# Pinning the two products that spread the tokens' 1/rms to their place in the code, 64 products later in TensorE's order

## The chip, the cores and the metric

One core of a Trainium2 chip runs the whole program. The metric is the device time of one execution in microseconds; the time before is the median of three runs, and a profiled execution stands beside them. The core's engines each have a queue of instructions of their own: TensorE (PE, matrix products; its weight loads are listed as PEld), VectorE (DVE), ScalarE (ACT), GpSimd (POOL) and SyncE (SP), which here issues nearly all transfers.

## What is computed

One residual block over 256 tokens of 2048 channels: an RMS norm, one wide input projection, an mLSTM branch and a pooling branch, gates, projections, an RMS norm and the residual add. What matters here is how the first norm is done:

```python
def _rmsnorm(x, w):
    xf = x.astype(jnp.float32)
    y = xf * lax.rsqrt(jnp.mean(xf * xf, axis=-1, keepdims=True) + RMS_EPS)
    return (y * w.astype(jnp.float32)).astype(x.dtype)

h = _rmsnorm(x, norm_pre_w[l])
proj = jnp.einsum('bsd,de->bse', h, w_in[l])
(q, k, v, o_g, z_a, i_pre, f_pre, u_b, z_b, g_a, g_b) = _partition(proj)
```

The kernel multiplies the weights with x unnormed (only scaled by the channel weights) and multiplies each token's result by its 1/rms afterwards.

## The kernel before

Every fp32 operand is split into a high and a low part (`hi_lo`: ACT casts the high part, `wh` from `raw`, at L62; DVE subtracts it to get the low part `wl`, at L63), and each product is made of three: high with high, low with high, high with low. Weights come in tiles of 1 MB (`raw`, three buffers), two halves each; `wh` and `wl` have four buffers.

`tok_block` makes results with tokens on the partitions, `chan_block` with channels on the partitions. `chan_block` goes through two tiles, that is four halves; for each half it writes eight products of `wh` (L143) and eight of `wl` (L145) and then calls `step()`, which moves every generator in the list `side` on by one `yield`. The side work is thereby strewn between the halves in the order of the code.

The start of the kernel: the first `tok_block` (L428) has 16 steps, through which `stats()` only counts. Then `so0` is copied out of PSUM (L432), `gates()` and `pool_weights()` join the list, and eight `chan_block`s follow (L435). Meanwhile `stats()` fetches x, squares and sums it on ACT (L245), adds the sums on DVE (L249, L192) and raises them to -1/2 on POOL (L193): `rstd`, one number per token, tokens on partitions. `stats_bc()` turns it into `rstd_bc`, the same numbers along the free axis on all partitions: a diagonal matrix `dg` from the identity and `rstd` (L261, DVE), a product of a matrix of ones with it (L262, one for each half of the tokens), and a copy from PSUM (L263, DVE). `rstd_bc` is read by `half_sum` (L409), through which every result of `chan_block` goes, and by `gates()` (L298). The flag `ready` lets `pooling` and `pool_gate` begin. `rstd` itself is read by others too: L573 scales the first two tiles `g` with it on ACT.

The order in an engine's queue is not simply the order of the code. A scheduler builds it from a plan of its own: at each point it takes the instruction that stands earliest in the code among those which its plan holds ready. So an instruction may stand in a queue ahead of others that come before it in the code, when the plan had these wait for something. In the order that results, the two products of L262 (written behind eight halves of `chan_block`) stand behind two, and five of the sixteen products of `gates()` (L286, written behind ten halves) follow at once; the other eleven stand behind ten. On the chip each engine works through its queue with the waits that its operands need.

## Time and profile before

| | |
|---|---|
| median of 3 runs | 978.75 us (978.57 to 978.86) |
| the profiled execution | 978.46 us |
| its span, first to last instruction | 976.7 us |
| TensorE busy | 965.9 us (99%) |
| VectorE busy | 630.6 us (65%) |
| ScalarE busy | 495.1 us (51%) |
| GpSimd busy | 14.5 us (1%) |

The durations all come from the one profiled execution; its own time is what they add up to. A row of a timeline gives the start and the length of an instruction, or of a run of like instructions (x8), in microseconds from the start of the span, then engine, line, operation and operands; in brackets the time that the engine stood idle before it and what ended that wait. Matrix products overlap: the length of one is longer than the distance to the next.

### The profile page before, as it was taken

How to read it: one execution, taken by the hardware profiler on the slowest of the kernel's cores; microseconds unless marked ns; L12 is line 12 of the kernel's file. 1: busy time of each engine (PE TensorE's matmuls, PEld its weight loads, DVE VectorE, ACT ScalarE, POOL GpSimd, SP SyncE). 2: the span in 40 equal slices, each digit the busy share in tenths (PEclk: the TensorE clock that was granted, in tenths of full speed). 3: DMA queues.
4: the chain of work that ended last, by engine and by line, in shares of the span. 5: the costliest groups of instructions: out<-in, count | busy, mean ns of one | idle time of the engine just before them, and what ended most of it. 6: DMA issues, size and time to landing. Idle time of an engine off the chain costs nothing.

```text
span 976.7 us, 12410 instructions
## 1 busy us (share of the span) xinstructions
PE 965.9 (99%) x4785; PEld 816.4 (84%) x4785; DVE 630.6 (65%) x938; ACT 495.1 (51%) x678; POOL 14.5 (1%) x35
## 2 busy tenths in 40 slices
PE   9999999999999999999999999999999999999996
PEld 6888888888888888888888888888888888888886
DVE  7699776677766867758677686554454455455563
ACT  7756444456644665546554475444444434443451
POOL 1000000000000000000000000000000000000001
PEclk9999999999999999999999999999999999999999
DMA  9755445544455435564555544555555555567542
GB/s 355 296 187 209 173 173 177 211 172 172 157 197 207 173 134 211 172 216 136 191 191 192 196 172 168 179 207 179 178 195 193 210 172 199 189 248 268 180 167 86
DMA packets 29306, 187.74 MB, mean 192 GB/s; under 512 B 3264, under 2 KB 3648, under 8 KB 8256
## 3 DMA queue, kind: packets, MB, share of 16 engines
q1 hardware_dynamic: 28816, 183.81, 52.6%
q10 hardware_dynamic: 432, 3.15, 0.8%
q8 instruction: 37, 0.61, 0.2%
q14 instruction: 21, 0.17, 0.0%
HBM read 184.85 MB, written 2.10 MB: 191 GB/s over the span
## 4 chain that ended last, share of the span: by engine, by line
PE 60%; issue 38%; ACT 1%; POOL 0%; DMA 0%; DVE 0%; DVEq 0%; SPq 0%; POOLq 0%
PE acc L143 18%; PE acc L123 10%; PE acc L124 10%; PE acc L126 10%; PE acc L145 9%; PE sm L72 1%; PE sm L71 1%; PE sm L73 1%; ACT xw L245 0%; PE sm L286 0%; DMA xw<-in_xw 0%; PE sm L559 0%; DVE xr L677 0%; PE sm L508 0%; POOL xr L675 0%
## 5 line engine op out<-in xcount | busy, mean ns | idle before, releaser
L63 DVE TENSOR_TENSOR wl<-raw,wh 128x1024 fp32r<-128x1024 f32 x328 | 398.5, 1223 | 263.6 <-ACT wh L62 263.4
L62 ACT CAST wh<-raw 128x1024 fp32r<-128x1024 f32 x328 | 342.3, 1050 | 370.4 <-PE acc L124 251.9
L123 PE MATMUL acc<-wh,xc 128*128 128x512 f32 x640 | 251.2, 392 | 0.1
L124 PE MATMUL acc<-wh,xc 128*128 128x512 f32 x640 | 249.6, 390 | 0.0
L143 PE MATMUL acc<-xc,wh 128*128 128x512 f32 x768 | 192.5, 392 | 0.0
L126 PE MATMUL acc<-wl,xc 128*128 128x512 f32 x640 | 172.5, 389 | 0.0
L143 PEld LDWEIGHTS acc<-xc,wh 128*128 128x128 f32 x768 | 138.9, 189 | 25.6
L126 PEld LDWEIGHTS acc<-wl,xc 128*128 128x128 f32 x640 | 120.2, 188 | 25.2
L123 PEld LDWEIGHTS acc<-wh,xc 128*128 128x128 f32 x640 | 120.4, 188 | 24.7 <-ACT wh L62 1.0
L124 PEld LDWEIGHTS acc<-wh,xc 128*128 128x128 f32 x640 | 120.4, 188 | 23.9
L145 PEld LDWEIGHTS acc<-xc,wl 128*128 128x128 f32 x768 | 104.8, 190 | 7.5
L145 PE MATMUL acc<-xc,wl 128*128 128x256 f32 x768 | 107.1, 282 | 0.0
L123 PE MATMUL acc<-wh,y_h 128*128 128x512 f32 x128 | 49.8, 389 | 0.0
L124 PE MATMUL acc<-wh,y_l 128*128 128x512 f32 x128 | 49.8, 389 | 0.0
L473 DVE SCALAR_TENSOR_TENSOR cy<-pad,vec,cy 128x256 f32<-128x256 f32 x96 | 39.3, 477 | 0.0
L123 PE MATMUL acc<-wh,m_h 128*128 128x512 f32 x96 | 37.6, 391 | 0.0
L124 PE MATMUL acc<-wh,m_l 128*128 128x512 f32 x96 | 37.4, 389 | 0.0
L126 PE MATMUL acc<-wl,y_h 128*128 128x512 f32 x128 | 34.2, 389 | 0.0
L123 PEld LDWEIGHTS acc<-wh,y_h 128*128 128x128 f32 x128 | 24.0, 188 | 5.0
L124 PEld LDWEIGHTS acc<-wh,y_l 128*128 128x128 f32 x128 | 24.0, 188 | 5.0
L126 PEld LDWEIGHTS acc<-wl,y_h 128*128 128x128 f32 x128 | 24.0, 188 | 5.0
L126 PE MATMUL acc<-wl,m_h 128*128 128x512 f32 x96 | 25.7, 389 | 0.0
(197 smaller groups left out, 771.6 us busy)
## 6 DMA issues: line engine op xcount, KB each, us to landing
raw<-in_wx SPq DMA_DIRECT2D x76, 1024.0 KB, 4.7
raw<-in_wq SPq DMA_DIRECT2D x44, 1024.0 KB, 4.8
raw<-in_wpm SPq DMA_DIRECT2D x16, 1024.0 KB, 4.7
raw<-in_wo SPq DMA_DIRECT2D x16, 1024.0 KB, 4.9
raw<-in_wpp SPq DMA_DIRECT2D x8, 1024.0 KB, 4.7
xw<-in_xw SPq DMA_DIRECT2D x15, 384.0 KB, 6.0
raw<-in_wq SPq DMA_DIRECT2D x8, 512.0 KB, 8.1
xw<-in_x SPq DMA_DIRECT2D x4, 512.0 KB, 8.3
```

The lines of the kernel that those rows point to most:

```text
L62: nc.scalar.copy(hi, src)
L63: nc.vector.tensor_tensor(lo, src, hi.bitcast(F32), op=ALU.subtract)
L71: nc.tensor.matmul(ps, lh, rh, start=start, stop=False)
L72: nc.tensor.matmul(ps, ll, rh, start=False, stop=False)
L73: nc.tensor.matmul(ps, lh, rl, start=False, stop=stop)
L123: nc.tensor.matmul(ps[t], st_h(k, t), wh[:, cols], start=k == 0, stop=False)
L124: nc.tensor.matmul(ps[t], st_l(k, t), wh[:, cols], start=False, stop=False)
L126: nc.tensor.matmul(ps[t], st_h(k, t), wl[:, cols], start=False, stop=k == n - 1)
L143: nc.tensor.matmul(ps[c], wh[:, cols], xc[:, k], start=k == 0, stop=False)
L145: nc.tensor.matmul(ps[c][:, 1], wl[:, cols], xc[:, k, 0], start=False, stop=k == KT - 1)
L473: nc.vector.scalar_tensor_tensor(y, pad[:, 1 + j : 1 + j + T], cw[:, j : j + 1], y, op0=ALU.mult, op1=ALU.add)
```

## The change

`stats()` now yields once instead of three times before it calls `stats_bc()`, so the latter is traced behind six halves of `chan_block` instead of eight, and `ready` is set there too. And the first of the two products is passed to `keep_in_program_order`, which adds an edge to the instruction traced last before it on the same engine: in TensorE's queue it has to stand behind it. The edge orders the queue and is no wait on a semaphore.

```diff
@@ stats()
         rsqrt_mean(rstd, ms, D)
-        for _ in range(3):
-            yield 1
+        yield 1
         stats_bc()
         ready.append(1)
@@ stats_bc()
         for t in range(2):
             dg = sp.tile([P, P], F32, name="dg", bufs=2)
             nc.vector.tensor_scalar(dg, ident, rstd[:, t : t + 1], None, op0=ALU.mult)
-            nc.tensor.matmul(pb[:, t * P : (t + 1) * P], ones_f, dg, start=True, stop=True)
+            i = nc.tensor.matmul(pb[:, t * P : (t + 1) * P], ones_f, dg, start=True, stop=True)
+            if t == 0:
+                tc.keep_in_program_order(i)
         nc.vector.tensor_copy(rstd_bc, pb[:, :T])
```

## Rows read from the trace of the kernel before

**Rows 1.** The page's head and first part: busy time of each engine.

```profile
span 976.7 us, 12410 instructions
PE 965.9 (99%) x4785; PEld 816.4 (84%) x4785; DVE 630.6 (65%) x938; ACT 495.1 (51%) x678; POOL 14.5 (1%) x35
```

**Rows 2.** TensorE's waits, whole span: for whom, us in total, times, longest.

```profile
PE sm L262 <- DVE dg L261: 1.6, 1, 1.6
PE sm L166 <- DVE zeros L161: 1.2, 1, 1.2
```

**Rows 3.** Timeline of TensorE, 32 to 40 us.

```profile
32.10 1.11 PE L145 MATMUL acc<-xc,wl 128*128 128x256 f32 x8
34.84 0.71 PE L262 MATMUL sm<-dg,ones_f 128*128 128x128 f32 x4 [1.63 <-DVE dg L261]
35.31 1.41 PE L286 MATMUL sm<-xc,gc 128*128 128x512 f32 x5
36.55 2.00 PE L143 MATMUL acc<-xc,wh 128*128 128x512 f32 x8
38.39 1.12 PE L145 MATMUL acc<-xc,wl 128*128 128x256 f32 x8
39.34 2.00 PE L143 MATMUL acc<-xc,wh 128*128 128x512 f32 x8
```

**Rows 4.** Timeline of VectorE, 30 to 36 us.

```profile
30.79 0.67 DVE L63 TENSOR_TENSOR gc<-gw,gc 128x64 fp32r<-128x64 f32 x4 [3.96 <-ACT gc L62]
...
34.50 0.48 DVE L261 TENSOR_SCALAR dg<-ident,rstd 128x128 f32<-128x128 f32 x2 [0.82 <-POOL rstd L193]
35.59 0.42 DVE L263 COPY rstd_bc<-sm 128x256 f32<-128x256 f32 x1 [0.61 <-PE sm L262]
```

**Rows 5.** Timeline of ScalarE, 34 to 36 us.

```profile
34.50 0.72 ACT L573 ACTIVATE g<-g,rstd 128x512 f32<-128x512 f32 x1 [1.21 <-POOL rstd L193]
35.13 1.04 ACT L62 CAST wh<-raw 128x1024 fp32r<-128x1024 f32 x1
```

**Rows 6.** Transfers issued from 22.2 to 23.0: median us to landing.

```profile
raw<-in_wq SPq DMA_DIRECT2D x1, 512.0 KB, 8.2
```

**Rows 7.** Timeline of TensorE's weight loads, around 36 us.

```profile
36.32 1.81 PEld L143 LDWEIGHTS acc<-xc,wh 128*128 128x128 f32 x8
```

**Rows 8.** Timelines of ScalarE and TensorE, the kernel's first split products.

```profile
4.58 0.62 ACT L62 CAST wh<-xw 128x512 fp32r<-128x512 f32 x1 [0.78 <-DMA xw<-in_xw]
...
5.25 0.80 PE L123 MATMUL acc<-wh,xc 128*128 128x512 f32 x1
5.85 0.46 PE L124 MATMUL acc<-wh,xc 128*128 128x512 f32 x1
```

**Rows 9.** Timeline of TensorE, 52 to 62 us.

```profile
52.35 1.12 PE L145 MATMUL acc<-xc,wl 128*128 128x256 f32 x8
53.31 2.00 PE L143 MATMUL acc<-xc,wh 128*128 128x512 f32 x8
...
58.89 2.72 PE L286 MATMUL sm<-xc,gc 128*128 128x512 f32 x11
```

**Rows 10.** Timeline of VectorE, 43 to 55 us.

```profile
43.84 1.22 DVE L63 TENSOR_TENSOR wl<-raw,wh 128x1024 fp32r<-128x1024 f32 x1 [0.48 <-ACT wh L62]
44.99 0.75 DVE L409 TENSOR_TENSOR u<-u,rstd_bc 128x256 f32<-128x256 f32 x2
...
47.34 2.35 DVE L63 TENSOR_TENSOR pw_l<-raw,pw_h 128x1024 fp32r<-128x1024 f32 x2
49.61 0.68 DVE L63 TENSOR_TENSOR pd_l<-pd,pd_h 128x512 fp32r<-128x512 f32 x1
50.21 4.71 DVE L63 TENSOR_TENSOR wl<-raw,wh 128x1024 fp32r<-128x1024 f32 x4
```

**Rows 11.** Timeline of ScalarE, 47 to 50 us.

```profile
47.45 0.62 ACT L62 CAST pd_h<-pd 128x512 fp32r<-128x512 f32 x1 [1.67 <-DVE pd L379]
47.98 1.99 ACT L62 CAST wh<-raw 128x1024 fp32r<-128x1024 f32 x2
```

## The prediction

> **What bounds the kernel now.** I read the page's first part, then TensorE's waits over the whole span, then the timelines of the engines around the one wait that is left. TensorE (PE) is busy for 965.9 of 976.7 us [rows 1]; no other engine comes near. Its waits over the whole span are two: 1.2 us at the very start, and 1.6 us in front of the pair of products of line 262 [rows 2]. So whatever the change can give lies in that hole, and whatever it can cost is a new hole somewhere else.

> I call the 16 products of one half tile of `chan_block` a unit (8 of L143, then 8 of L145) and number them u1, u2, ... from 27.5 us. A unit takes 2.79 us (u3 at 36.55, u4 at 39.34), of which the L145 half, from 38.39, is 0.95. u2's L145 half starts at 32.10, so the next product could have gone at 32.10 + 0.95 = 33.05. The pair starts at 34.84: 1.79 us of PE are lost. Then come five of the sixteen gate products (L286), and u3 starts at 36.55 [rows 3]. The pair waits for `dg`, and `dg` sat waiting for `rstd`, GpSimd's power, until 34.50 [rows 4].

> **The second wait behind the first.** Does the hole close if the pair goes elsewhere? u3 needs its own `wh`. ScalarE (ACT) casts it from 35.13 to 36.17, and the entry ahead of it in ACT's queue is L573, the scaling of `g` with `rstd`: ACT stood idle for 1.21 us, from 33.29 on, for that same `rstd`, and started L573 at 34.50 [rows 5]. It did not wait for the raw tile of u3: that was issued between 22.2 and 23.0 and landed 8.2 us later, by 31.2 [rows 6]. So u3 cannot start before 36.17 wherever the pair stands, as long as ACT's order is kept, and nothing in the change touches an ACT instruction ahead of that cast. On this step the forecast turns: the `rstd` that holds the pair holds, by way of ACT's queue, the next unit too.

> That ACT does not step over L573 is read from those rows. [...]

> **The change part by part.**
> (a) The pair moves. In the code `stats_bc` ran after u8, but its products float up to behind u2; now it is traced after u6, and the edge holds the first product behind u6's last one, 64 products later. The pair takes 34.84 to 35.31, 0.47 us of PE [rows 3], and takes the same after u6, where `dg` will be 12 us old, so no wait: +0.47 at the new place.
> (b) u3's start. Its first weight load goes at 36.32 now [rows 7], behind the gate products. After a wait for ACT the nearest row is the kernel's start: cast done at 4.58 + 0.62 = 5.20, load and product at 5.25, the next product 0.60 later, at 5.85 [rows 8]. So u3's load would go at 36.17 + 0.05 = 36.22 and its second product, by that row, at 36.82, against 36.55 + 0.23 = 36.78 now: +0.04. If the first product is as quick as now, the load's 36.32 - 36.22 is won: -0.10. I take -0.05, between them.
> (c) The gate products. They were ready before the pair (`gc` is written by 31.46 [rows 4]) and yet stand behind it, so in the plan that made the order there was no idle time ahead of the pair that they could have filled; the place that opens is the pair's own. Each takes (36.55 - 35.31)/5 = 0.25 us [rows 3], so 0.47 holds two. Each one more in the hole is one fewer behind u10, where eleven stand now [rows 9]: -0.25 each. How long the pair is in the plan no row shows; between none and twice its measured length that is 0 to 4 products, 0 to -0.99. I take 2, by the measured length: -0.50.
> (d) VectorE (DVE). `rstd_bc` (L263) is copied 0.75 us after the pair starts, now at 35.59 [rows 3, 4]. The pair will start at some 47.6 (u7 starts two units ahead of u9, at 53.31 - 2 x 2.79 = 47.7 [rows 3, 9]), so the copy moves to 48.35 and ends at 48.78, 13 us later. Queued behind it are its readers: from the first L409 to the end of the chain that makes `pd` it is 44.99 to 47.34, 2.35 us [rows 10], so `pd` is ready at 51.1 instead of 47.4. On ACT its cast (0.62) waits for it, and behind that the casts of u9 and u10 [rows 11]: 51.1 + 0.62 + 1.04 = 52.8 for u9, which starts at 53.31 + 0.4 = 53.7 [rows 9]. 0.9 us to spare: 0. On DVE the `wl` of u9 now starts at 50.21 [rows 10] and is wanted by u9's L145 half, at 53.31 + (38.39 - 36.55) + 0.4 = 55.5 [rows 3, 9]. If both `pw_l` casts (2.35) and `pd_l` (0.68) stay ahead of it, it ends at 51.1 + 2.35 + 0.68 + 1.22 = 55.35: just in time; if `pw_l` is done while DVE waits (45.1 to 48.3 lies free for it), at 53.0. SP's raw tiles go into buffers that those casts free: u11's follows the `wl` of u8 (done at 45.06 now), and u11 is wanted only behind the gate products of 58.89. Cost taken: 0.
> (e) `ready` is set two steps earlier in the code, so the first `pooling` is traced two steps sooner. Its accumulators are freed by L407 and L408, which don't read `rstd_bc`, so PE gets its PSUM back as before: 0.

> Sum: -0.05 + 0.47 - 0.50 = -0.08 us. Bounds: -0.10 + 0.47 - 0.99 = -0.62, and +0.04 + 0.47 = +0.51. The profiled execution took 978.46 (the span 976.7 and 1.76 around it); the median of the three runs is 978.75, 0.29 above. 978.46 - 0.08 + 0.29 = 978.67; I write 978.7, with a range of its own, the bounds, of 978.1 to 979.3.

> **Rivals.**
> 1. The hole closes. If ACT's order comes out with the cast of u3 ahead of L573 (its tile landed by 31.2, ACT is free at 33.29 [rows 5, 6]), `wh` is there at 34.35, gate products bridge 33.05 to then, and all 1.79 us are won: 978.75 - 1.79 = 976.95. The same if some nine or more gate products fill the hole. For it: the data is there. Against it: the plan put L573 first though it stands far later in the code, so in the plan the tile was not there yet, and no edit changes that. This is also about the ceiling: PE has no other hole.
> 2. One product stays. The edge is on `t == 0` alone. If the second product may go ahead of the first, it stands where the pair stands and waits for the second `dg`, done at 34.50 + 0.48 = 34.98, 0.14 later than PE's start there now: the hole stays, 978.75 + 0.1 = 978.85. Against it: both write the same tile `pb`, and they stand in code order now.
> 3. Slower, through DVE. The copy of `rstd_bc` waits at DVE until 48.35 for the pair. If the plan puts the `wl` of u8 (now begun at 43.84 [rows 10]) behind the copy, its readers and `pw_l`, it ends at 48.78 + 2.35 + 2.35 + 0.68 + 1.22 = 55.4, and u8's L145 wants it at 52.35 + 0.4 = 52.7 [rows 9]: PE stands 2.7 us, 978.7 + 2.7 = 981.4. It decides once more than 52.7 - 48.78 - 1.22 = 2.7 us of other DVE work stands between the copy and that cast. Against it: that cast begins 3.9 us ahead of u7 now. A smaller stall of the kind would still count as no change.

> **How the numbers follow.** A difference under 0.2% (1.96 us) is about what a measurement of this kernel cannot tell from none. Forecast 0.68; hole closed 0.15; one product stays 0.08; slower through DVE, or through another queue that the new plan orders worse, 0.09. Forecast and rival 2 hold 0.76, so the range reaches to the closed hole, with 0.15 of spread between runs: 976.8 to 979.3. The closed hole lies 0.17 us inside the limit for faster (976.79); I give 0.03 of its 0.15 to the far side. Faster 0.03, same 0.68 + 0.08 + 0.12 = 0.88, slower 0.09.

> **What would show it.** In the profile after: L262 in PE's order behind 96 products of `chan_block`, with no wait in front; some seven L286 behind u2, nine behind u10; PE idle from about 34.8 to 36.2, put down to ACT's `wh` and no longer to `dg`; L573 still ahead of u3's cast; u3 within 0.15 us of 36.55; L263 near 48.4, with DVE waiting for PE before it, some of that filled by `pw_l`; no other wait on PE. It is wrong if u3 starts near 34.8 (rival 1), if an L262 stands at 35 (rival 2), or if PE waits for a `wl` or `wh` between 47 and 60 us (rival 3).

## The result, and the profile after

The changed kernel takes 981.43 us (median of 14 executions, 979.73 to 982.41), the kernel before 978.72 (14, 978.21 to 979.39); ratio 1.0024, 95% interval 1.0016 to 1.0032. It is slower by 0.24%, against a forecast of no change at 978.7 and a range that ended at 979.3. The slower rival put the time almost there (981.4), but by a mechanism that is not in the trace.

The executions of the changed kernel fall into two groups: five from 979.73 to 980.28 with a granted clock of 0.998 over the span, and nine from 980.98 to 982.41 with 0.995 to 0.997. The profiled one (981.44, span 979.7) belongs to the second.

TensorE's waits over the whole span, to be read against [rows 2]:

```profile
PE acc L143 <- ACT wh L62: 3.0, 1, 3.0
PE sm L166 <- DVE zeros L161: 1.2, 1, 1.2
```

The wait of the pair (L261 in this kernel) for `dg` is gone. In its place stands one nearly twice as long, of u3's first product for ScalarE's `wh`. The timeline of TensorE, against [rows 3] and [rows 9]:

```profile
32.14 1.11 PE L145 MATMUL acc<-xc,wl 128*128 128x256 f32 x8
36.25 3.42 PE L143 MATMUL acc<-xc,wh 128*128 128x512 f32 x8 [3.00 <-ACT wh L62]
39.47 1.41 PE L145 MATMUL acc<-xc,wl 128*128 128x256 f32 x8
40.71 2.02 PE L143 MATMUL acc<-xc,wh 128*128 128x512 f32 x8
...
49.09 0.60 PE L261 MATMUL sm<-dg,ones_f 128*128 128x128 f32 x4
49.45 2.11 PE L143 MATMUL acc<-xc,wh 128*128 128x512 f32 x8
...
60.73 3.89 PE L287 MATMUL sm<-xc,gc 128*128 128x512 f32 x16
64.46 1.98 PE L143 MATMUL acc<-xc,wh 128*128 128x512 f32 x8
```

Three things are to be seen. Between u2's end at 33.1 and u3 at 36.25 there is no product at all: the five gate products that stood there are now behind u10, where all sixteen stand (L287, 60.73). u3, the unit that starts at 36.25, takes 40.71 - 36.25 = 4.46 us instead of 2.79. And the pair is where it was to go, behind u6, without a wait. ScalarE's order is what it was in [rows 5]:

```profile
33.13 0.19 ACT L245 ACTIVATION_READ_ACCUMULATOR xw<-xw 128x1 f32 x1
34.54 0.72 ACT L574 ACTIVATE g<-g,rstd 128x512 f32<-128x512 f32 x1 [1.21 <-POOL rstd L193]
35.16 1.03 ACT L62 CAST wh<-raw 128x1024 fp32r<-128x1024 f32 x1
```

Why u3 is slow is in the windows of that stretch (start:end, its length, then busy time of PE, PEld, DVE, ACT and POOL with counts; the figure behind POOL's is the granted clock as a share of full speed, then DMA share and GB/s):

```profile
33.20:36.25 3.05, 0.05 (x1) 0.00 (x1) 0.83 (x5) 1.84 (x5) 0.71 (x1) 1.00 0.55 218
36.25:37.25 1.00, 1.00 (x3) 0.84 (x4) 1.00 (x1) 1.00 (x2) 0.00 (x0) 0.73 0.00 0
37.25:38.25 1.00, 1.00 (x4) 0.72 (x3) 0.67 (x2) 1.00 (x2) 0.00 (x0) 0.50 0.00 0
38.25:39.25 1.00, 1.00 (x4) 0.81 (x3) 1.00 (x2) 1.00 (x2) 0.00 (x0) 0.50 0.00 0
39.25:40.71 1.46, 1.46 (x10) 1.36 (x9) 1.46 (x2) 1.41 (x2) 0.00 (x0) 0.70 0.58 90
```

The clock is up through the idle stretch itself (1.00) and falls just after products have begun again: 0.73 in the first microsecond of them, 0.50 in the next two. From 40.25 to 40.71 it is at 1.00 again. Behind that unit nothing on TensorE waits any more, and the rest of the span keeps the distance: u11 starts at 64.46 instead of 61.45, 3.01 later, and the span is 3.0 longer. The row of before for u11:

```profile
61.45 2.00 PE L143 MATMUL acc<-xc,wh 128*128 128x512 f32 x8
```

The late copy of `rstd_bc` is there, as forecast, and VectorE interleaves its readers with the `wl` casts (against [rows 10]):

```profile
49.74 0.42 DVE L264 COPY rstd_bc<-sm 128x256 f32<-128x256 f32 x1 [1.73 <-PE sm L261]
50.08 1.21 DVE L63 TENSOR_TENSOR wl<-raw,wh 128x1024 fp32r<-128x1024 f32 x1
51.21 0.75 DVE L410 TENSOR_TENSOR u<-u,rstd_bc 128x256 f32<-128x256 f32 x2
```

### The profile page after: what moved, and what is told of

Its sections match the earlier page's. It is cut to its first block, busy times and chain, and to the rows that moved or that the text cites. A ratio compares the mean times of both kernels' runs of the same rounds, so it can differ in the third digit from the quotient of the medians.

```text
span 979.7 us, 12415 instructions
## 1 busy us (share of the span) xinstructions
PE 967.4 (99%) x4785; PEld 817.6 (83%) x4785; DVE 630.5 (64%) x938; ACT 496.2 (51%) x679; POOL 14.5 (1%) x35
## 3 DMA queue, kind: packets, MB, share of 16 engines
q1 hardware_dynamic: 28816, 183.81, 52.7%
## 4 chain that ended last, share of the span: by engine, by line
PE 60%; issue 38%; ACT 1%; POOL 0%; DMA 0%; DVE 0%; DVEq 0%; SPq 0%; ACTq 0%; POOLq 0%
PE acc L143 18%; PE acc L123 10%; PE acc L124 10%; PE acc L126 10%; PE acc L145 9%; PE sm L72 1%; PE sm L71 1%; PE sm L73 1%; ACT xw L245 0%; PE sm L287 0%; DMA xw<-in_xw 0%; PE sm L560 0%; DVE xr L678 0%; PE sm L509 0%; POOL xr L676 0%
## 5 line engine op out<-in xcount | busy, mean ns | idle before, releaser
L143 PE MATMUL acc<-xc,wh 128*128 128x512 f32 x768 | 194.1, 395 | 3.0 <-ACT wh L62 3.0
L143 PEld LDWEIGHTS acc<-xc,wh 128*128 128x128 f32 x768 | 139.5, 190 | 28.9 <-ACT wh L62 3.2
L145 PEld LDWEIGHTS acc<-xc,wl 128*128 128x128 f32 x768 | 105.2, 191 | 7.6
L145 PE MATMUL acc<-xc,wl 128*128 128x256 f32 x768 | 107.3, 283 | 0.0
L126 PE MATMUL acc<-wl,y_h 128*128 128x512 f32 x128 | 34.2, 389 | 0.0
```

The source lines that it names most:

```text
L126: nc.tensor.matmul(ps[t], st_h(k, t), wl[:, cols], start=False, stop=k == n - 1)
L143: nc.tensor.matmul(ps[c], wh[:, cols], xc[:, k], start=k == 0, stop=False)
L145: nc.tensor.matmul(ps[c][:, 1], wl[:, cols], xc[:, k, 0], start=False, stop=k == KT - 1)
```

## The experiments

The theory (A): the loss is the hole in front of u3. Its end is set by ScalarE's order; the gate products have left it with the pair; and after the idle stretch of 3.00 us the clock falls. The rival (B): the loss comes from the copy of `rstd_bc`, 14 us later, through the queues of VectorE and ScalarE. The times of before beside them are medians of 29, 27 and 15 executions on the same chips: 978.57, 978.52 and 978.64. Line numbers shift with each edit: the pair stands at L261 or L262, the gate products at L283 to L288. Starts shift too, from one execution to the next: u2's L145 half starts between 32.10 and 32.64 in the traces shown here. So waits and distances are compared, and starts only where u2 lies alike.

**The edge or the yields.** First the edge alone, in the kernel before:

```diff
-            nc.tensor.matmul(pb[:, t * P : (t + 1) * P], ones_f, dg, start=True, stop=True)
+            i = nc.tensor.matmul(pb[:, t * P : (t + 1) * P], ones_f, dg, start=True, stop=True)
+            if t == 0:
+                tc.keep_in_program_order(i)
```

> The edge alone, with the three yields of before: the pair then stands behind u8. Theory A (the loss is the hole in front of u3: the pair and with it the five gate products have left it, u3 still waits for ScalarE, and the long idle stretch lets TensorE's clock fall): the hole is the same as in the changed kernel, 33.1 to 36.25, none of the sixteen gate products in it; about 981.4 us, or near 980.0 in executions in which the clock holds. Theory B (the loss comes from the late copy of rstd_bc, through the queues of VectorE and ScalarE): the copy comes another 5.6 us later, at about 55.3, so the time rises above 982.5. Theory C (the yields do it): as before, 978.7.

981.59 us (981.48 to 982.76, 6 executions), ratio 1.0031 [1.0019, 1.0043], and the clock fell in all six, to judge by their mean clocks over the span (0.995 and 0.996); in the profiled one it is 0.50 from 37.50 to 40.50. The copy of `rstd_bc` comes 6.5 us later still, and it costs nothing: the time is that of the changed kernel, not above 982.5. B falls here. The hole, in its timeline of TensorE:

```profile
36.33 2.86 PE L143 MATMUL acc<-xc,wh 128*128 128x512 f32 x8 [3.00 <-ACT wh L62]
```

and the copy, in its timeline of VectorE:

```profile
56.22 0.42 DVE L265 COPY rstd_bc<-sm 128x256 f32<-128x256 f32 x1
```

Then the yields alone: the changed kernel without the edge.

```diff
-            i = nc.tensor.matmul(pb[:, t * P : (t + 1) * P], ones_f, dg, start=True, stop=True)
-            if t == 0:
-                tc.keep_in_program_order(i)
+            nc.tensor.matmul(pb[:, t * P : (t + 1) * P], ones_f, dg, start=True, stop=True)
```

> The changed kernel without the edge: only the yields, one instead of three. Theory A: the pair floats up behind u2 again and five gate products with it: order and hole as before, 978.7 us. If the earlier ready and the earlier pooling cost anything by themselves, more.

A single execution, 979.04 us (before 978.52, between 978.07 and 979.14). Pair, five gate products and hole are as before, all of it 0.54 later (the pair at 35.38 instead of 34.84, u3 at 37.09 instead of 36.55); u2's L145 half, ahead of the hole, is already 0.54 late, at 32.64 instead of 32.10. TensorE's timeline:

```profile
35.38 0.71 PE L261 MATMUL sm<-dg,ones_f 128*128 128x128 f32 x4 [1.63 <-DVE dg L260]
35.85 1.40 PE L285 MATMUL sm<-xc,gc 128*128 128x512 f32 x5
37.09 2.01 PE L143 MATMUL acc<-xc,wh 128*128 128x512 f32 x8
```

So the edge makes the loss; the yields by themselves leave the order and the hole as they were, and cost nothing that one execution can tell from the spread.

**Only the pair moved.** The changed kernel with the gate products where they stood before, five behind u2 and eleven behind u10:

```diff
-        for _ in range(3):
-            yield 1
+        yield 1
         for i, g4 in enumerate(gc):
             hi_lo(...)
-        for _ in range(6):
-            yield 1
         pg = small()
         for k in range(KT):
-            nc.tensor.matmul(
+            if k == 5:
+                for _ in range(8):
+                    yield 1
+            i = nc.tensor.matmul(
                 pg, ...
             )
+            if k in (0, 5):
+                tc.keep_in_program_order(i)
```

> The changed kernel with the gate products where they stood before: five behind u2 (and held there), eleven behind u10. So the only difference from before in TensorE's order is the pair, behind u6 instead of u2. Theory A: hole 33.05 + 5 x 0.233 = 34.2 to 36.25, 2.0 us, no fall of the clock; u3 0.3 earlier than before, the pair +0.36 behind u6: 978.8 us, no change. Theory B (late rstd_bc): 981.4, as the copy of rstd_bc is as late as in the changed kernel.

980.41 us (978.66 to 981.39, 11 executions), ratio 1.0014 [1.0005, 1.0023]. Three executions are at 978.66, 978.72 and 978.85: the 978.8 of theory A, which settles the order part. In the other eight, from 980.02 on, the clock fell, to judge by their times and by their mean clock over the span (0.995 to 0.997, against 0.998 and 0.999 in the three); A had not expected that for a hole this short. The profiled one (980.58), the one of the eight that was traced, shows it, first in TensorE's timeline, then in the windows (columns as above):

```profile
33.37 1.32 PE L287 MATMUL sm<-xc,gc 128*128 128x512 f32 x5
36.53 3.02 PE L143 MATMUL acc<-xc,wh 128*128 128x512 f32 x8 [1.84 <-ACT wh L62]
39.35 1.80 PE L145 MATMUL acc<-xc,wl 128*128 128x256 f32 x8
```

```profile
34.70:36.50 1.80, 0.00 (x0) 0.00 (x0) 0.48 (x2) 1.68 (x3) 0.09 (x1) 1.00 0.23 93
36.50:37.50 1.00, 0.97 (x4) 0.84 (x5) 0.99 (x1) 1.00 (x2) 0.00 (x0) 0.98 0.00 0
37.50:38.50 1.00, 1.00 (x3) 0.69 (x3) 0.66 (x2) 1.00 (x2) 0.00 (x0) 0.50 0.00 0
```

With eight instead of five (`k == 8` and `(0, 8)` in the edit):

> As the kernel with five gate products back in the hole, but with eight: idle from 33.05 + 8 x 0.233 = 34.9 to 36.25, 1.3 us, near the 1.1 us of the kernel with the later scalings, whose clock held in all executions. Theory A: u3 still starts at 36.25 behind ScalarE, three products fewer stand behind u10, -0.70 against the 978.7 of the five-product kernel with its clock up: 978.0 us, all executions within 0.5 of it. If products in the hole are not worth 0.233 each, 978.7; if a shorter idle stretch does not save the clock, executions near 979.7 as well.

978.10 us (977.34 to 978.75, 11 executions), ratio 0.9994 [0.9985, 1.0003]: 0.6 below the 978.7 of the five-product kernel with its clock up, for the 0.70 expected, and no group at 979.7. (The spread is 1.4, a little wider than the 0.5 to either side that was expected.) So a gate product in the hole is worth what it takes, and with a wait of 1.15 us the clock held, to judge by the times and the mean clocks (0.997 and 0.998). TensorE's timeline:

```profile
33.22 2.01 PE L287 MATMUL sm<-xc,gc 128*128 128x512 f32 x8
36.38 2.14 PE L143 MATMUL acc<-xc,wh 128*128 128x512 f32 x8 [1.15 <-ACT wh L62]
```

**Why the gate products left.** The changed kernel, with the pair's result in a PSUM tile that exists already:

```diff
-        pb = small()
+        pb = warm
         for t in range(2):
             dg = sp.tile([P, P], F32, name="dg", bufs=2)
```

> The changed kernel, with the pair writing into the PSUM tile that the start already holds (warm) instead of a new one, so that the gate products' tile no longer comes behind the pair's in the order in which tiles of that pool are given out. Theory A with the tile order as the reason: the sixteen gate products go into the hole, 33.05 + 16 x 0.233 = 36.8, longer than u3's wait (36.2); no wait of TensorE left. Against before: u3 0.25 later, the pair +0.36 behind u6, eleven gate products fewer behind u10 -2.56: about -1.9, 976.9 us, clock never down. Theory B (late rstd_bc): rstd_bc is as late as in the changed kernel, so at least 2 us stay, 979 us or more. If the tile order is not the reason, the gate products stay behind u10 and the time is 981.4.

977.07 us (976.87 to 977.64, 11 executions), ratio 0.9983 [0.9974, 0.9992]. All sixteen are in the hole, and the clock is 1.00 in every window from 30.00 to 41.50. TensorE's timeline:

```profile
33.41 3.89 PE L287 MATMUL sm<-xc,gc 128*128 128x512 f32 x16
37.14 1.98 PE L143 MATMUL acc<-xc,wh 128*128 128x512 f32 x8
39.20 1.22 PE L145 MATMUL acc<-xc,wl 128*128 128x256 f32 x8
```

The edit changes nothing of what the gate products read or when that is ready, only which tile the pair takes. So it was the tile: `pb` and the gate products' `pg` come from one pool, `small()`; the plan gave `pg` out only after `pb`; and `pb` waits, by the edge, for u6. (That the sixteen then stand at their own place in the code, behind u10, and not directly behind the pair would fit a plan without idle time in between; no run tests that.) Against before on the same chip the gain is 1.50 us, for the expected 1.9. u3 takes 3.12 us (u4 at 40.26) instead of 2.79: on VectorE the first reduction of the gate products' result now stands ahead of u3's `wl`, and u3's L145 half begins at 39.20 instead of 38.98 (37.14 + 1.84). And the pair costs 0.47 instead of the 0.36 that was put in. VectorE's timeline, then that of the weight loads:

```profile
37.34 0.68 DVE L295 TENSOR_REDUCE row<-sm 8x256 f32<-8x512 f32 x1 [1.99 <-PE sm L287]
37.95 3.47 DVE L63 TENSOR_TENSOR wl<-raw,wh 128x1024 fp32r<-128x1024 f32 x3
39.20 1.01 PEld L145 LDWEIGHTS acc<-xc,wl 128*128 128x128 f32 x8 [0.51 <-DVE wl L63]
```

**ScalarE's order.** The changed kernel with the two scalings of `g` held to their place in the code:

```diff
-            nc.scalar.activation(s, po[t], AF.Sigmoid, scale=rstd[:, t : t + 1])
+            i = nc.scalar.activation(s, po[t], AF.Sigmoid, scale=rstd[:, t : t + 1])
+            if j == 0:
+                tc.keep_in_program_order(i)
```

> The changed kernel with one thing moved on ScalarE: the two scalings of g with rstd are held to their place in the code, so they no longer stand ahead of u3's cast. Theory A: the cast of u3 begins at 33.3, where ScalarE is free, its wh is there at 34.35, the hole ends at 34.4 instead of 36.25, too short for the clock to fall. Against before: u3 2.15 earlier, pair +0.36, five gate products +1.16 behind u10: 978.1 us. If u3 waits for its transfer or anything else than ScalarE's order, the hole and the time stay at 981.4.

978.05 us (977.76 to 978.45, 11 executions), ratio 0.9996 [0.9987, 1.0005]: as expected to 0.1. ScalarE casts u3's tile the moment it is done with the squares. Its timeline:

```profile
33.54 0.19 ACT L245 ACTIVATION_READ_ACCUMULATOR xw<-xw 128x1 f32 x1
33.63 4.84 ACT L62 CAST wh<-raw 128x1024 fp32r<-128x1024 f32 x5
```

u3 follows at once, and the clock is 1.00 in every window from 30.00 to 41.50. TensorE's timeline:

```profile
34.72 2.14 PE L143 MATMUL acc<-xc,wh 128*128 128x512 f32 x8 [1.06 <-ACT wh L62]
```

The transfer was not what u3 waited for; the scaling in front of its cast was.

**The clock alone.** The changed kernel with thirteen products of zeros in the hole, whose result nothing reads:

```diff
+    def filler():
+        for _ in range(17):
+            yield 1
+        for _ in range(13):
+            i = nc.tensor.matmul(warm, zeros[:, 0:P], zeros, start=True, stop=True)
+            tc.keep_in_program_order(i)
+
     side.append(stats())
+    side.append(filler())
```

> The changed kernel, with thirteen products of zeros (bf16, 128x512, their result is never read) held behind u2: 13 x 0.216 = 2.8 us of work that does nothing but keep TensorE busy in the hole. Theory A: u3 still starts at 36.25, but the clock stays at its upper level, u3 takes 2.79 instead of 4.46 us: 980.0 us in every execution, no spread to 981.5. If the fall of the clock has nothing to do with the idle stretch, the executions spread from 979.7 to 982.4 as with the changed kernel. Theory B: 981.4.

979.91 us (979.45 to 980.28, 11 executions), ratio 1.0011 [1.0002, 1.0020]: one group, where the changed kernel has two. The thirteen products take 2.98 us, for the expected 2.8. u3 starts at the same 36.24, u4 follows after 2.92 us instead of 4.46, and the clock is 1.00 in every window from 30.00 to 41.50 (TensorE's timeline):

```profile
33.08 2.98 PE L433 MATMUL sm<-zeros 128*128 128x512 bf16 x13
36.24 2.14 PE L143 MATMUL acc<-xc,wh 128*128 128x512 f32 x8 [0.18 <-ACT wh L62]
38.22 1.10 PE L145 MATMUL acc<-xc,wl 128*128 128x256 f32 x8
39.16 2.00 PE L143 MATMUL acc<-xc,wh 128*128 128x512 f32 x8
```

**Is it the unbroken stretch?** The kernel before with all gate products held behind u10, the pair left in the hole:

```diff
         for k in range(KT):
-            nc.tensor.matmul(
+            i = nc.tensor.matmul(
                 pg, ...
             )
+            if k == 0:
+                tc.keep_in_program_order(i)
```

> The kernel before, with the sixteen gate products held behind u8 to u10 and the pair left where it was, behind u2. So the idle time in front of u3 is 33.05 to 34.84 and 35.3 to 36.25, 2.7 us in all, parted by the pair. Theory A with an unbroken idle stretch as the reason for the clock: no fall; u3 0.3 earlier, five gate products +1.16 behind: 979.6 us in every execution. If the sum of idle time brings the clock down: spread up to 981.2.

980.83 us (979.38 to 981.51, 11 executions), ratio 1.0021 [1.0012, 1.0030]. Three executions, the profiled one among them, are at 979.38 to 979.66, the 979.6 of theory A. In eight, from 980.54 on, the clock fell, to judge by their times and their mean clock (0.996 to 0.997, against 0.998 in the three); none of the eight was traced. So, by these times, the 0.47 us of the pair in the middle of the idle time do not keep the clock up, and that part of A does not hold. It also shows that the gate products alone, moved out without the pair, cost most of what the change costs. The profiled execution's timeline of TensorE, with two waits and the pair between:

```profile
34.86 0.71 PE L262 MATMUL sm<-dg,ones_f 128*128 128x128 f32 x4 [1.63 <-DVE dg L261]
36.23 2.11 PE L143 MATMUL acc<-xc,wh 128*128 128x512 f32 x8 [0.66 <-ACT wh L62]
```

**Filling the hole from the start.** The kernel before, neither edge nor yields of the change, but with all gate products traced behind u2 and the first held there:

```diff
-        for _ in range(3):
-            yield 1
+        yield 1
         for i, g4 in enumerate(gc):
             hi_lo(...)
-        for _ in range(6):
-            yield 1
         pg = small()
         for k in range(KT):
-            nc.tensor.matmul(
+            i = nc.tensor.matmul(
                 pg, ...
             )
+            if k == 0:
+                tc.keep_in_program_order(i)
+        for _ in range(8):
+            yield 1
```

> The kernel before without edge and with its three yields, but the gate products traced behind u2 and held there, ahead of the pair, which floats up as before. Theory A: sixteen products fill 33.05 to 36.8, the pair follows without a wait (dg is ready at 35), u3 starts at 37.1: no idle time left, 978.72 - 1.79 = 976.95 us. So the work that fills the wait is what gains, not the place of the pair. If the pair had to move for the gain, 978.7 or more.

976.73 us (976.26 to 976.91, 11 executions), ratio 0.9981 [0.9972, 0.9990], 1.79 below before: the ceiling of the prediction, and the fastest of all. TensorE's timeline:

```profile
33.11 3.89 PE L283 MATMUL sm<-xc,gc 128*128 128x512 f32 x16
36.83 0.60 PE L262 MATMUL sm<-dg,ones_f 128*128 128x128 f32 x4
37.19 2.10 PE L143 MATMUL acc<-xc,wh 128*128 128x512 f32 x8
```

The pair still floats up behind u2; its `dg` has long been ready at 36.83, so it waits for nothing, and u3's `wh` is there too.

## Why the prediction was wrong, step by step

| term | forecast, us | measured, us | from |
|---|---|---|---|
| pair behind u6 | +0.47 | +0.47 | 0.36 to u7, and u7's first half 2.11 instead of 2.00 |
| u3 behind ScalarE | -0.05 | -0.19 | u4 at 39.15 with the clock up, 39.34 before |
| gate products | -0.50 | +1.17 | 60.73 to 64.46 for sixteen, 58.89 to 61.45 for eleven |
| sum, clock up | -0.08 | +1.45 | five executions: 980.13 - 978.72 = +1.41 |
| the clock | none | +1.56 | u4 at 40.71 instead of 39.15; nine executions of 14 |

The 39.15 is u3's start at 36.25, 2.79 for the unit and 0.11 for its first half behind a wait (2.11 instead of 2.00 in the kernel before with the gate products held behind u10).

**Right.** What bounds the kernel; that the hole does not close because `rstd` holds ScalarE's queue too, and with it u3's `wh` (with the later scalings its wait is 1.06 us instead of 3.00); u3's place, 36.25 against a forecast load at 36.22; the pair's price; and that the 14 us delay of `rstd_bc` costs nothing on VectorE or ScalarE, in the changed kernel and with the edge alone even 6.5 us later. Rival 3 had the number, 981.4, by luck, and is refuted: no `wl` or `wh` is waited for behind u3. Its chance also covered "another queue that the new plan orders worse", which is near to what happened on TensorE, but without a mechanism or a price. Rival 2 did not occur, the second product follows the first. Rival 1's price was right: with the hole filled, 976.73 against 976.95.

**The step that failed: (c).** From "they were ready and yet stand behind the pair" it concluded that the plan had no idle time ahead of the pair. The other reading was that something besides their operands held them behind it. It was their PSUM tile, which the plan gives out after the pair's (shown by the pair in `warm`). So the bound of "0 to 4 products more" began at the wrong place: the five that stood there were held to the pair, and the true change was five fewer. That turned -0.50 into +1.17, and the sum from none to +1.45.

**What followed from it.** With no product in the hole TensorE stood idle from 33.1 to 36.25 instead of the 34.8 to 36.2 of the forecast, and in nine executions of 14 the clock fell, for another 1.56. The prediction had no term for the clock: in the trace of before it is at full speed at the hole and behind it (1.00 from 32.00 to 42.13), and the hole that it expected was shorter than the present one (1.4 us for 1.79). With the hole filled by work of no use the second group disappears, so the fall is caused by the hole. In the traced execution of the changed kernel the clock was down for most of a unit of work (0.50 in u3) behind a wait of 3.00 us; in the traced one with five gate products a shorter wait, of 1.84 us, was enough. For the hole of 1.4 us that the prediction expected, the trace of before gave no reason for a rival: there the clock held through a longer one. What a hole of 3.0 us does to it, the one that step (c) missed, no trace had shown by then.

What stays open: what decides whether the clock falls. It held in all executions with 1.1 us of wait in front of u3, fell in eight of 11 with one wait of 1.84, in eight of 11 with 1.63 and 0.66 parted by the pair, in nine of 14 and six of six with 3.0; and in the kernel before, with 1.63 and then seven products before u3, no second group shows (one execution of 29 stands apart at 980.44, with a mean clock of 0.998, and was not traced). Only one execution of each was traced: in the others the fall is read from times and mean clocks, and its place was not seen.

## What to carry to other kernels

Before a waiting instruction is moved, ask what else waits for the same producer on other queues, and what useful work stands in the shelter of the wait; here that was u3's cast in ScalarE's queue and five gate products. In an order that a planner makes, work that is ready and yet stands behind another may be held there by a buffer rather than by its data: a place in a shared pool moves with the instruction that takes it. And the cheaper answer to a wait that cannot be shortened is to bring other ready work in front of it (976.73), not to take the waiting work away (981.43).
